# Rounded and low halves of weight chunks interleaved element by element for the stationary operand

## The chip, the cores and the metric

The kernel runs on one core of one Trainium2 chip. The metric is the device time of one execution in microseconds; lower is better. The chip multiplies on TensorE (PE in the profile), which loads a 128x128 stationary operand (the weight load, PEld) and then streams a moving operand of up to 512 columns past it. VectorE is DVE, ScalarE is ACT, GpSimd is POOL, and SyncE (SP) issues most transfers.

## The reference, cut to what matters

One decoder layer on 512 positions with a model width of 1024, in float32:

```python
h = rms_norm(x, norm1_g) * (1 + scale1) + shift1
z = h @ w_in      # [gMLP u | gMLP v | q | k | v | indexer q | indexer k | head weights | gate A | gate B]
y_a = chunked_gmlp(gelu(a_u), gelu(a_v), ...)
y_b = dsa_attention(q, k, v, qi, ki, wi)         # top-k keys of 512, 8 heads
merged = sigmoid(g_a) * (y_a @ w_proj_a) + sigmoid(g_b) * (y_b @ w_proj_b)
x = x + gate1 * (merged @ w_out)
h2 = rms_norm(x, norm2_g) * (1 + scale2) + shift2
f_g, f_u = split(h2 @ w_ffn_in)                   # 2 x 2816 columns
x = rms_norm(x + gate2 * ((silu(f_g) * f_u) @ w_ffn_out), final_norm_g)
```

The shifts, scales and gates are rows of `silu(c) @ w_ada + b_ada`.

## The kernel before, in words

Every large product is done in three passes to keep float32 accuracy. A float32 operand is split in a rounded half `hi` (a copy by ScalarE into the type fp32r) and a low half `lo` (the original minus `hi`, by VectorE or GpSimd). `mm3` then issues three matmuls: hi x hi, hi x lo and lo x hi, at lines 107, 108 and 109, so that these three lines carry nearly all matmuls, and a group of instructions is known by its tiles. In `mm3` the first pair is the stationary operand (128 columns are loaded), the second the moving one.

Weights come as a stream of chunks of 128 partitions x 1024 float32 (512 KB). `issue` starts the transfer of a chunk into one of three `raw` buffers, `prep` writes its halves into the next of three `hi` and three `lo` buffers (lines 156, 157, 163 and 167), and `get` and `ensure` hold the stream two chunks ahead of the matmuls. An entry of the stream is prepared in order. Among the weights stand rows of `w_ada` (`mod_row`, tile `mraw`): each is multiplied and summed on VectorE at line 255, and in the middle of the kernel all of them use one buffer.

The stages, in order of time, with the tiles that show in the rows:

- 16 to 49 us: eight chunks `W1` of 768 columns are stationary against `h`, six output tiles at a time (`k<-h`, `q<-h`, lines 606 to 610). Here GpSimd makes the low halves in pieces (line 165).
- 49 to 104 us: `W_Q` (`pb<-h`, by `opt_b`) with the chunk stationary and 384, later 512 columns of `h` moving; between them `W_VKI` (`pv`) with the chunk moving.
- 105 to 154 us: `W_AV` (`pav`), the chunk moving.
- 154 to 296 us: `W_AU`, `W_GA`, `W_PA` by `opt_b`, the chunk stationary, `h` or `y` moving (`pb<-h`, `pb<-y`). Beside it run the gMLP mixing (`mix`; `mix_ev` makes `y`), the top-k on VectorE (`sco`) and the `w_ada` rows.
- 297 to 370 us: attention, step by step (`at_step`), with the matmuls of `W_GB` (`pgb<-h`, chunk stationary) put between its steps.
- 371 to 414 us: `W_PB` (`pb<-yb`, chunk stationary), then the output projection (`po`).
- 457 to 671 us: the first FFN product by a Strassen-like scheme (`sprod`, tile `R`): 256 columns of `tb` or `h2` move, the chunk is stationary. Of the units `q`, the even ones take the buffers `hi` and `lo` three pairs at a time (`s_pair`), the odd ones other tiles (`sx`).
- 671 to 776 us: the second FFN product (`zprod`, tile `pfo`): the activations `za` are stationary, the chunk moves.

Where tiles lie is part of the design. All `raw`, `hi` and `lo` buffers before the change begin at 0 modulo 256 bytes of a partition, and so do `h`, `y`, `yb` and `za`. The moving operands of `sprod` are placed at 192 modulo 256 by `at_line(..., 192)`, its stationary ones lie at 0 or 128. `at_line` and small unused tiles (`fill`) hold these offsets.

Of the kernel before, what the change touches and what calls it, by code (L numbers as in the profile page):

```python
# [9 lines left out]
F32 = mybir.dt.float32  # L10
F32R = mybir.dt.float32r
# [5 lines left out]
S = 512  # L17
# [41 lines left out]
def block_kernel(ctx: ExitStack, tc: tile.TileContext, x, x_t, w_in,  # L59
# [3 lines left out]
    T, V, A, P, SY = nc.tensor, nc.vector, nc.scalar, nc.gpsimd, nc.sync  # L63
    ctx.enter_context(tc.manual_schedule())
    tiny = ctx.enter_context(tc.tile_pool(name="tiny", bufs=1))
    base = ctx.enter_context(tc.tile_pool(name="base", bufs=1))
# [6 lines left out]
    def packed(ap, name):  # L73
        at, o = {}, 0
        for k0, nk, cols_ in _plan()[name]:
            m = 128 * nk * sum(n for _, n in cols_)
            at[k0, nk, cols_] = slice(o, o + m)
            o += m
        return lambda k0, nk, cols_: ap[at[k0, nk, cols_]].rearrange("(p m) -> p m", p=128)

    w_in, w_ffn_in, w_ffn_out = (packed(*a) for a in ((w_in, "w_in"), (w_ffn_in, "w_ffn_in"), (w_ffn_out, "w_ffn_out")))
# [4 lines left out]
    def at_line(pool, tag, dims, dt, name, off=0):  # L86

        n = math.prod(dims)
        pad = 256 if tag == "E6" else (256 - HOME[tag]) % 256 or 192 if tag in HOME else 0
        t = pool.tile([128, n + pad // 4], dt, name=name, tag=tag, bufs=1)  # L90
        o = (off - HOME.get(tag, 0)) % 256 // 4
        letters = "abcd"[:len(dims)]
        return t[:, o:o + n].rearrange(f"p ({' '.join(letters)}) -> p {' '.join(letters)}",
                                       **dict(zip(letters[1:], dims[1:])))
# [4 lines left out]
    def f(ap):  # L99
        return ap.bitcast(F32)  # L100
# [11 lines left out]
    stream, wseq, chunk = [], [], {}  # L112
# [2 lines left out]
    last_raw = {}  # L115
    mrot = [0]

    def add_w(src, kts, c0, n, lo=None, where=None):
        stream.append(dict(kind="w", src=src, kts=kts, c0=c0, n=n, lo=lo or V, where=where))
        wseq.append(len(stream) - 1)  # L120
        return len(stream) - 1

    def add_m(dma, fn, early=False, mid=True):
        stream.append(dict(kind="m", fn=fn, dma=dma, early=early, mid=not early and mid))
        return len(stream) - 1
# [23 lines left out]
    def prep(i):  # L149
        e = stream[i]  # L150
        if e["kind"] == "m":
            e["fn"](e["raw"])
            return
        m = len(e["kts"]) * e["n"]
        if e["where"] is None:
            hi = base.tile([128, 1024], F32R, name="hi", tag="hi", bufs=3)
            lo = base.tile([128, 1024], F32R, name="lo", tag="lo", bufs=3)
        elif isinstance(e["where"], tuple):
            hi, lo = (at_line(base, t, (1024,), F32R, "wx") for t in e["where"])
        else:  # L160
            t = at_line(ffn[0], e["where"], (2, 1024), F32R, "wx", 128 * (e["where"] in ("E1", "E6")))
            hi, lo = t[:, 0], t[:, 1]
        A.activation(hi[:, :m], e["raw"][:, :m], AF.Copy)  # L163
        if e["lo"] == "later":
            e["do"] = lambda E=V, c=slice(0, m): E.tensor_sub(lo[:, c], e["raw"][:, c], f(hi[:, c]))
        else:
            e["lo"].tensor_sub(lo[:, :m], e["raw"][:, :m], f(hi[:, :m]))  # L167
        chunk[i] = (e["view"](hi), e["view"](lo))

    def ensure(upto):  # L170
        upto = min(upto, len(stream) - 1, st["limit"] - 1)
        while True:
            for i in range(st["prep"], min(st["prep"] + 16, len(stream), st["limit"])):
                if "raw" in stream[i]:
                    continue
                if room(i):
                    issue(i)
                elif stream[i]["kind"] == "w" or not stream[i]["mid"]:
                    break
            if st["prep"] > upto:  # L180
                break
            prep(st["prep"])
            st["prep"] += 1

    def room(i):
        e = stream[i]
        if i in last_raw:
            return True
        pend = [stream[k] for k in range(st["prep"], i) if k not in last_raw]
        if e["kind"] == "m" and e["early"]:  # L190
            return sum(p["kind"] == "m" for p in pend) < 8
        if e["kind"] == "m" and e["mid"]:
            return all(p["kind"] == "w" for p in pend) and len(pend) <= 1
        return sum(p["kind"] == "w" or not (p["early"] or p["mid"]) for p in pend) < RAWB


    def get(i, ahead=2):
        k = wseq.index(i)
        ensure(wseq[min(k + ahead, len(wseq) - 1)])
        return chunk[i]  # L200
# [10 lines left out]
    mid = mid_stack.enter_context(tc.tile_pool(name="mid", bufs=1))  # L211
# [5 lines left out]
    vmid = mid_stack.enter_context(tc.tile_pool(name="vmid", bufs=1))  # L217
    ffn = []

    for k in range(8):  # L220
        at_line(base, f"S2_{k}", (1024,), F32, "home")
    base.tile([128, 16], F32, name="fill")
    vmid.tile([128, 16], F32, name="fill")

    def s2pair(k, dt=F32R, name="s2"):
        return at_line(base, f"S2_{k}", (2, S), dt, f"{name}{k}")
# [51 lines left out]
    def group(src, c0, n=256, K=8, mods=None, pool=False, where=None, nm=1, mraw="A2"):  # L278
        ids = []
        for k0 in range(0, K, 4):  # L280
            ids.append(add_w(src, list(range(k0, min(K, k0 + 4))), c0, n,
                             P if pool == 2 or pool and k0 % 8 == 0 else V, where.pop(0) if where else None))
            for _ in range(nm if isinstance(nm, int) else nm[k0 // 4]):
                m = next(mods, None) if mods is not None else None
                if m is not None:
                    add_m(*m, mid=mods is mm_ and mraw)
        return ids

    W1M, W1 = [], []
    mods1 = [iter([mod_row(0, kt), mod_row(1, kt)]) for kt in range(8)]  # L290
    for c in "00w11w22w33w44w55w66w77w":
        if c == "w":
            W1.append(add_w(w_in, [len(W1)], ((3072, 256), (2048, 512)), 768, "later"))
        else:
            W1M.append(add_m(*next(mods1[int(c)]), True))
    W_Q = [group(w_in, 3584 + 256 * g) for g in range(2)]
# [100 lines left out]
    def x_kt(kt):  # L397
        return xts[kt // 4][:, kt % 4]
# [5 lines left out]
    for i in range(4):  # L404
        t = base.tile([128, D], F32, name=f"x{i}", tag=f"X{i}", bufs=1)
# [20 lines left out]
    def t512(name, dt=F32):  # L426
        return base.tile([128, 512], dt, name=name, tag="t512", bufs=3)
# [5 lines left out]
    def split(hi, lo, src):  # L433
        A.activation(hi, src, AF.Copy)
        V.tensor_sub(lo, src, f(hi))
# [74 lines left out]
    def stage_E(kt):  # L510
        g, sh, v = G1[:, 1, kt:kt + 1], G1[:, 0, kt:kt + 1], x_kt(kt) if kt else xp[0]
        if kt:
            A.activation(hT[kt][0], v, AF.Identity, scale=g, bias=sh)
        else:
            V.tensor_scalar(hT[kt][0], v, g, sh, op0=OP.mult, op1=OP.add)
        hf = hfs[kt] = t512("hf")
        A.activation(hf, v, AF.Identity, scale=g, bias=sh)
# [40 lines left out]
    def copy_x(c):  # L558
        for kt in (1, 2):
            A.activation(x_kt(kt)[:, c], xp[kt][:, c], AF.Copy)  # L560
# [12 lines left out]
    A.activation(rb, rbp, AF.Copy)  # L573
    copy_x(slice(256, 512))
    ensure(W1[0])
    stage_E(0)

    def low_w1(kt):
# [17 lines left out]
    for kt in range(8):  # L596
        hi, lo = chunk[W1[kt]]
# [5 lines left out]
        hh, hl = hT[kt]  # L603
# [93 lines left out]
    kin = mid.tile([128, 4, 128], F32, name="kin", tag="A2", bufs=1)  # L697
    wi = mid.tile([128, 4, 8], F32, name="wi")
    bst = vmid.tile([128, 4, 24], F32, name="bst", tag="L", bufs=1)
    mid.tile([128, 32], F32, name="fill")  # L700
    mv = tiny.tile([128, 4, 2], F32, name="mv")
    rki = sm[:, 8:12]

# [244 lines left out]
    for h in range(2):  # L948
        pb = [bank(k, "pav") for k in range(4)]
        for i in W_AV[h]:  # L950
# [10 lines left out]
            hi, lo = get(i)  # L961
# [328 lines left out]
    mT, om, ow, oraw = {}, {}, {}, {}  # L1290
# [11 lines left out]
    def o_w(key, src):  # L1302
        if key in OW:
            ow[key] = tuple((vmid if t[0] == "v" else mid).tile([128, 2, S], F32R, name="ow", tag=t, bufs=1)
                            for t in OW[key])
        else:
            ow[key] = tuple(base.tile([128, 2, S], F32R, name=t, tag=t, bufs=3) for t in ("hi", "lo"))
        split(*ow[key], oraw[src])

    def o_sub(o, a, b):  # L1310
# [24 lines left out]
    def pb_evac(g):  # L1335
        def ev(pb):
# [11 lines left out]
            if g == 2:  # L1348
                m_low(4)
        return ev  # L1350

    O_STEPS = [[lambda: o_w("B11", "B11")],
               [lambda: o_sub("B11", "B12", "B11")],
               [lambda: o_w("T1", "B11")],
# [103 lines left out]

    def s_pair(q, n):
        if q % 2 == 0:  # L1460
            return (base.tile([128, 4, 2, 128], F32R, name="hi", tag="hi", bufs=3),
                    base.tile([128, 4, 2, 128], F32R, name="lo", tag="lo", bufs=3))
        if n < 2:
            t = at_line(ffn[0], f"E{n}", (2, 4, 2, 128), F32R, "sx", 128 * (n == 1))
            return t[:, 0], t[:, 1]
        return tuple(at_line(base, f"S2_{2 + e}", (4, 2, 128), F32R, "sx") for e in range(2))
# [111 lines left out]
    for half in range(2):  # L1578
        for h in range(2):
# [5 lines left out]
            for n_, i in enumerate(W_O[2 * h:2 * h + 2]):  # L1585
                hi, lo = chunk[i]
# [158 lines left out]
    for half in range(2):  # L1745
        o = slice(half * 256, (half + 1) * 256)
        for w in range(2):
            for ci, i in enumerate(W_F[w]):
                hi, lo = chunk[i]
# [250 lines left out]
    for tk in range(2):  # L2000
        for z in range(2) if tk else (None,):
# [4 lines left out]
            n = c.stop - c.start  # L2006
# [78 lines left out]
```

## Time and profile before

| | before |
|---|---|
| median of the runs | 785.41 us |
| runs | 784.4 and 786.42 us |
| span of the profiled execution | 783.3 us |
| instructions in it | 12307 |

The span goes from the first to the last instruction of one profiled execution. The profile gives no other time for that execution: its own time is its span with what lies around it, and the two timed runs are 1.1 and 3.1 us longer than the span. A row of the timeline has start, length, engine, line, operation, tiles and count; the length of a matmul in it contains its way through the array, so the pace of matmuls is read from start to start, never from the lengths.

### The profile page before, as it was taken

The numbers are of one execution on the slowest core, as the hardware profiler recorded it, in microseconds if no ns is written. First come the engines' busy times: TensorE is split into PE (matmuls) and PEld (weight loads), VectorE is DVE, ScalarE is ACT, GpSimd is POOL, SyncE is SP. The second block draws the span as 40 slices with busy tenths as digits, with TensorE's granted clock in tenths as the row PEclk, the third lists the DMA queues.
The fourth block names the chain that finished last, engine by engine and source line by source line (L and its number), as shares of the span: only waits on it lengthen the run. The fifth ranks groups of instructions, "written<-read, shape, count | busy, mean of one in ns | idle before, by whom it ended". The sixth has DMA issues, their size and how long they took to land.

```text
span 783.3 us, 12307 instructions
## 1 busy us (share of the span) xinstructions
PE 774.1 (99%) x4579; PEld 688.5 (88%) x4579; DVE 666.6 (85%) x1128; ACT 427.3 (55%) x757; POOL 179.0 (23%) x234
## 2 busy tenths in 40 slices
PE   8999999999999999999999999999999999999996
PEld 7899888888888888988888899999999999888885
DVE  7989788887889559986697879989999888998877
ACT  6664445423332246666546577655566666676654
POOL 4870222312344412100020000313132223000001
PEclk8999999999999999999999999999999999999999
DMA  9953252332435558627682603879897967556762
GB/s 345 416 187 125 82 168 75 135 99 89 132 123 206 210 188 225 180 75 265 220 248 33 209 1 109 253 231 300 268 254 230 270 205 210 162 187 206 219 216 112
DMA packets 51277, 146.24 MB, mean 187 GB/s; under 512 B 13969, under 2 KB 14737, under 8 KB 51218
## 3 DMA queue, kind: packets, MB, share of 16 engines
q1 hardware_dynamic: 41408, 114.35, 42.2%
q0 software_dynamic: 9232, 30.15, 15.2%
q10 hardware_dynamic: 578, 0.95, 0.3%
q8 instruction: 36, 0.59, 0.3%
q14 instruction: 23, 0.19, 0.1%
HBM read 140.97 MB, written 27.27 MB: 215 GB/s over the span
## 4 chain that ended last, share of the span: by engine, by line
PE 81%; DVE 9%; DMA 6%; ACT 2%; issue 1%; SPq 0%; POOL 0%; POOLq 0%; DVEq 0%; ACTq 0%
PE R L107 8%; PE R L109 8%; PE R L108 8%; PE pb L108 5%; PE pb L109 5%; PE pb L107 5%; PE pfo L109 4%; PE pfo L107 4%; PE pfo L108 4%; DMA mraw<-in_w_shsc_dram 4%; DVE mraw L255 2%; PE pav L109 2%; PE pav L108 2%; PE pav L107 2%; PE po L109 2%; PE po L107 2%
## 5 line engine op out<-in xcount | busy, mean ns | idle before, releaser
L163 ACT ACTIVATE hi<-raw 128x1024 fp32r<-128x1024 f32 (+4 forms) x106 | 107.4, 1014 | 94.4 <-PE pb L108 38.9
L167 DVE TENSOR_TENSOR lo<-raw,hi 128x1024 fp32r<-128x1024 f32 (+2 forms) x73 | 85.4, 1171 | 24.0 <-ACT hi L163 23.6
L167 POOL TENSOR_TENSOR lo<-raw,hi 128x1024 fp32r<-128x1024 f32 x25 | 59.9, 2398 | 106.7 <-ACT hi L163 101.2
L107 PE MATMUL pb<-h,hi 128*128 128x512 f32 (+1 forms) x192 | 73.6, 383 | 0.0
L108 PE MATMUL pb<-h,hi 128*128 128x512 f32 (+1 forms) x192 | 73.0, 380 | 0.0
L109 PE MATMUL pb<-h,lo 128*128 128x512 f32 (+1 forms) x192 | 73.0, 380 | 0.0
L108 PE MATMUL pfo<-lo,za 128*128 128x512 f32 (+1 forms) x144 | 55.2, 383 | 0.0
L109 PE MATMUL pfo<-hi,za 128*128 128x512 f32 (+1 forms) x144 | 55.2, 383 | 0.0
L107 PE MATMUL pfo<-hi,za 128*128 128x512 f32 (+1 forms) x144 | 55.2, 383 | 0.0
L255 DVE CUSTOM_DVE_ANT_0 mraw<-mraw,csb,cols 128x1024 f32<-128x1024 f32 x27 | 39.3, 1455 | 18.6 <-DMA mraw<-in_w_shsc_dram 18.6
L389 POOL COPY sm<-sm 128x1 f32<-128x1 f32 x36 | 25.0, 696 | 92.3 <-ACT sm L388 92.2
L107 PE MATMUL R<-tb,hi 128*128 128x256 f32 x160 | 44.2, 276 | 0.0
L108 PE MATMUL R<-tb,hi 128*128 128x256 f32 x160 | 44.2, 276 | 0.0
L109 PE MATMUL R<-tb,lo 128*128 128x256 f32 x160 | 44.2, 276 | 0.0
L107 PE MATMUL R<-tb,sx 128*128 128x256 f32 x160 | 44.2, 276 | 0.0
L108 PE MATMUL R<-tb,sx 128*128 128x256 f32 x160 | 44.2, 276 | 0.0
L109 PE MATMUL R<-tb,sx 128*128 128x256 f32 x160 | 44.2, 276 | 0.0
L109 PEld LDWEIGHTS pb<-h,lo 128*128 128x128 f32 x192 | 36.0, 188 | 6.3
L108 PEld LDWEIGHTS pb<-h,hi 128*128 128x128 f32 x192 | 36.1, 188 | 6.0
L107 PEld LDWEIGHTS pb<-h,hi 128*128 128x128 f32 x192 | 36.1, 188 | 6.0
L369 POOL DMA_DIRECT2D wsum<-in_w_ffn_out_dram x24 | 19.6, 822 | 72.3 <-DMA wsum<-wsum 39.7
L108 PEld LDWEIGHTS pfo<-lo,za 128*128 128x128 f32 x144 | 27.1, 188 | 5.4
(395 smaller groups left out, 2563.2 us busy)
## 6 DMA issues: line engine op xcount, KB each, us to landing
raw<-in_w_ffn_in_dram SPq DMA_DIRECT2D x44, 512.0 KB
raw<-in_w_in_dram SPq DMA_DIRECT2D x40, 512.0 KB
wsum<-in_w_ffn_out_dram POOLq DMA_DIRECT2D x30, 512.0 KB, 7.5
mraw<-in_w_shsc_dram SPq DMA_DIRECT2D x27, 512.0 KB
raw<-wsum SPq DMA_DIRECT2D x20, 512.0 KB
s<-in_w_shsc_dram SPq DMA_DIRECT2D x14, 512.0 KB
raw<-in_w_ffn_out_dram SPq DMA_DIRECT2D x13, 512.0 KB
wsum<-wsum POOLq DMA_DIRECT2D x10, 512.0 KB, 5.9
```

The lines of the kernel that those rows point to most:

```text
L107: T.matmul(o, wh, rh, start=start, stop=False, **kw)
L108: T.matmul(o, wh, rlo, start=False, stop=False, **kw)
L109: T.matmul(o, wlo, rh, start=False, stop=stop, **kw)
L163: A.activation(hi[:, :m], e["raw"][:, :m], AF.Copy)
L167: e["lo"].tensor_sub(lo[:, :m], e["raw"][:, :m], f(hi[:, :m]))
L255: V.tensor_tensor_reduce(out=raw[:, c], in0=raw[:, c], in1=(csb if s > 1 else pc)[:, c], scale=scale, scalar=sums.pop(0), op0=OP.mult, op1 ...
L369: P.dma_start(wsum_at(n, c), src, max_dma_last_dim=4096, accum_op=OP.add)
L389: P.tensor_copy(t, t)
```

## The change

The three `hi` and three `lo` buffers become three buffers `hl` of 2048 elements with 16 more as padding (8256 bytes, that is 64 more than a multiple of 256), so that they begin at 0, 64 and 128 modulo 256. For chunks that are marked `still` (those of `W1` and of `group`, when they go through these buffers) `hi` has the even and `lo` the odd elements: an engine that writes or reads a half steps by 8 bytes, and a weight load reads 128 elements over 1024 bytes where it read 512 bytes. For all others `hi` is the first and `lo` the second 1024 elements of a buffer. Small unused tiles are moved so that later tiles of the pool keep their offsets.

```diff
+    def pair_tile():
+        return base.tile([128, 2064], F32R, name="hl", tag="hl", bufs=3)[:, :2048]
+
-    def add_w(src, kts, c0, n, lo=None, where=None):
+    def add_w(src, kts, c0, n, lo=None, where=None, still=False):
...
         if e["where"] is None:
-            hi = base.tile([128, 1024], F32R, name="hi", tag="hi", bufs=3)
-            lo = base.tile([128, 1024], F32R, name="lo", tag="lo", bufs=3)
+            t = pair_tile()
+            if e["still"]:
+                t = t.rearrange("p (m e) -> p m e", e=2)
+                hi, lo = t[:, :, 0], t[:, :, 1]
+            else:
+                hi, lo = t[:, :1024], t[:, 1024:]
...
     base.tile([128, 16], F32, name="fill")
-    vmid.tile([128, 16], F32, name="fill")
...
             ids.append(add_w(src, list(range(k0, min(K, k0 + 4))), c0, n,
-                             P if pool == 2 or pool and k0 % 8 == 0 else V, where.pop(0) if where else None))
+                             P if pool == 2 or pool and k0 % 8 == 0 else V, where.pop(0) if where else None, True))
...
-            W1.append(add_w(w_in, [len(W1)], ((3072, 256), (2048, 512)), 768, "later"))
+            W1.append(add_w(w_in, [len(W1)], ((3072, 256), (2048, 512)), 768, "later", still=True))
...
     ensure(W1[0])
+    base.tile([128, 16], F32, name="fill2")
...
-    mid.tile([128, 32], F32, name="fill")
+    mid.tile([128, 16], F32, name="fill")
...
-            ow[key] = tuple(base.tile([128, 2, S], F32R, name=t, tag=t, bufs=3) for t in ("hi", "lo"))
+            t = pair_tile().rearrange("p (e j n) -> p e j n", e=2, j=2)
+            ow[key] = (t[:, 0], t[:, 1])
...
         if q % 2 == 0:
-            return (base.tile([128, 4, 2, 128], F32R, name="hi", tag="hi", bufs=3),
-                    base.tile([128, 4, 2, 128], F32R, name="lo", tag="lo", bufs=3))
+            t = pair_tile().rearrange("p (h j e n) -> p h j e n", h=2, j=4, e=2)
+            return t[:, 0], t[:, 1]
```

## Rows read from the trace of the kernel before

**Rows 1.** The page: busy time by engine, and the chain that ended last.
```profile
PE 774.1 (99%) x4579; PEld 688.5 (88%) x4579; DVE 666.6 (85%) x1128; ACT 427.3 (55%) x757; POOL 179.0 (23%) x234
...
PE 81%; DVE 9%; DMA 6%; ACT 2%; issue 1%; SPq 0%; POOL 0%; POOLq 0%; DVEq 0%; ACTq 0%
```

**Rows 2.** Timeline of PE, 40.7 to 42.2 us, inside stage W1.
```profile
40.76 0.61 PE L606 MATMUL k<-h,hi 128*128 128x512 f32 x2
...
42.12 0.61 PE L608 MATMUL k<-h,lo 128*128 128x512 f32 x2
```

**Rows 3.** Windows: stretch, its us, each engine's busy us (instructions), PEclk, DMA, GB/s.
```profile
16.00:49.00 33.00, 33.00 (x145) 27.05 (x146) 29.21 (x41) 20.92 (x31) 29.81 (x49) 1.00 0.91 358
49.00:66.00 17.00, 17.00 (x100) 17.00 (x99) 16.66 (x30) 9.18 (x16) 5.75 (x12) 1.00 0.43 137
154.00:182.50 28.50, 28.50 (x132) 23.76 (x131) 23.82 (x39) 8.59 (x11) 5.94 (x4) 1.00 0.26 89
182.50:310.00 127.50, 127.50 (x594) 106.64 (x592) 100.57 (x226) 47.71 (x74) 44.81 (x26) 1.00 0.51 171
310.00:372.00 62.00, 61.86 (x376) 54.91 (x375) 51.81 (x155) 40.96 (x104) 6.06 (x12) 1.00 0.56 180
372.00:414.00 42.00, 42.00 (x187) 34.79 (x186) 34.07 (x44) 18.48 (x25) 5.65 (x10) 1.00 0.73 228
482.00:671.00 189.00, 189.00 (x1670) 189.00 (x1669) 174.17 (x237) 115.49 (x235) 48.19 (x74) 1.00 0.81 237
```

**Rows 4.** Timeline of PE near the end: 256 columns move, both operands at 0.
```profile
774.37 0.28 PE L107 MATMUL pfo<-hi,za 128*128 128x256 f32 x1
...
775.81 0.28 PE L107 MATMUL pfo<-wx,zl 128*128 128x256 f32 x1
```

**Rows 5.** Groups of weight loads by form: count, busy us, mean ns, idle before.
```profile
L107 PEld LDWEIGHTS pb<-h,hi 128*128 128x128 f32 x192 | 36.1, 188 | 6.0
...
L107 PEld LDWEIGHTS pfo<-hi,za 128*128 128x128 f32 x144 | 27.1, 188 | 5.3
...
L107 PEld LDWEIGHTS pgb<-h,hi 128*128 128x128 f32 x64 | 12.1, 188 | 2.5 <-ACT gb L1220 0.6
...
L107 PEld LDWEIGHTS pb<-y,hi 128*128 128x128 f32 x64 | 12.0, 188 | 2.4
...
L107 PEld LDWEIGHTS pb<-yb,hi 128*128 128x128 f32 x64 | 12.0, 188 | 2.5
...
L606 PEld LDWEIGHTS q<-h,hi 128*128 128x128 f32 x32 | 6.0, 188 | 1.3
...
L606 PEld LDWEIGHTS k<-h,hi 128*128 128x128 f32 x16 | 2.8, 188 | 1.1 <-ACT h L513 0.4 <-issue 0.3
```

**Rows 6.** The chain that ended last, in order of time, 182 to 311 us.
```profile
182.50 0.91 PE mix L984 x8
183.43 0.70 DVE y L990
...
227.18 4.30 DMA mraw<-in_w_shsc_dram
...
231.50 1.29 DVE mraw L255
...
309.84 0.56 ACT gb L1220
...
310.44 0.50 PE pgb L107
```

**Rows 7.** Groups that write or read the halves, by form: count, busy us, mean ns.
```profile
L163 ACT ACTIVATE hi<-raw 128x1024 fp32r<-128x1024 f32 x89 | 94.0, 1058 | 85.6 <-PE pb L108 38.9 <-PE pfo L109 18.6 <-issue 14.5
...
L167 DVE TENSOR_TENSOR lo<-raw,hi 128x1024 fp32r<-128x1024 f32 x64 | 78.1, 1221 | 23.1 <-ACT hi L163 22.8
...
L167 POOL TENSOR_TENSOR lo<-raw,hi 128x1024 fp32r<-128x1024 f32 x25 | 59.9, 2398 | 106.7 <-ACT hi L163 101.2 <-PE pb L108 4.5 <-POOL sco L768 0.9
...
L165 POOL TENSOR_TENSOR lo<-raw,hi 128x384 fp32r<-128x384 f32 x8 | 8.0, 1017 | 2.4 <-ACT hi L163 2.4
```

More of the change, by code (lines that the diff above doesn't have):

```diff
@@ L116, in block_kernel @@
     mrot = [0]
-    def add_w(src, kts, c0, n, lo=None, where=None):
-        stream.append(dict(kind="w", src=src, kts=kts, c0=c0, n=n, lo=lo or V, where=where))
+    def pair_tile():
+        return base.tile([128, 2064], F32R, name="hl", tag="hl", bufs=3)[:, :2048]
+    def add_w(src, kts, c0, n, lo=None, where=None, still=False):
+        stream.append(dict(kind="w", src=src, kts=kts, c0=c0, n=n, lo=lo or V, where=where, still=still))
         wseq.append(len(stream) - 1)
```

## The prediction

> **What bounds the kernel now.** I read the page first: TensorE is busy 99% of the span and holds 81% of the chain that ended last; VectorE has 9% of it and transfers 6% [rows 1]. So the first question is what sets TensorE's pace, and that is read from starts, not from lengths. In stage W1 six matmuls of 512 columns start between 40.76 and 42.12 us, 226.7 ns each [rows 2]. The granted clock there is 1.00, which is the level of 2.4 GHz [rows 3], and 512 columns at one column per cycle are 213.3 ns. Each matmul is 13.3 ns, or 32 cycles, over its columns. The same is seen with 256 columns (106.7 ns): near the end of the kernel, with both operands at 0 modulo 256 bytes, twelve matmuls take from 774.37 to 775.81 us, 120 ns each, again 13.3 over [rows 4]; in `sprod`, where the moving operand lies at 192, the stretch from 482 to 671 us holds 1670 in 189 us, 113.2 ns each, only 6.5 over [rows 3]. The two have the same number of columns, the same clock and the same kind of weight load. What differs is the address of the moving operand against that of the weights loaded beside it. I read this as two streams that meet in the same part of the memory: the moving one goes 4 bytes per cycle; a weight load of 128 columns fits into 113 ns in `sprod`, so it goes at about half of that, and the moving stream keeps overtaking it.
>
> The second question is where TensorE's pace sets the end. Up to the mixing at 182.50 us the chain is TensorE's; from the `y` at 183.43 on it runs through VectorE and the `mraw` transfers (4.30 us of transfer, then 1.29 us of line 255, and so on) and comes back to TensorE only at the `pgb` of 310.44, which had waited for ScalarE [rows 6]. That wait is 0.6 us in all [rows 5]. So from 182.5 to 310 us two chains are equally long: TensorE is busy in all 127.5 us [rows 3], but the other would not be shorter if it were faster.
>
> **The change part by part.** *The interleaved weight load.* It reads 1024 bytes in the time in which it read 512, so it moves at the bytes per cycle of the moving stream. Two streams of one speed don't overtake each other: they are apart for the whole load, or one is held once and they are apart after that. From the rows a matmul then costs between nothing and one meeting over its columns. The nearest row for one meeting is `sprod`'s 6.5 ns [rows 3], so the saving lies between 6.7 and 13.3 ns per matmul. With three buffers at three distances from the moving operand, which lies at 0, I expect some of each and take the middle, 10 ns, that is a pace of about 217 ns. The unseen lower end, a load that gets more expensive, is a rival below.
>
> The Trainium skill has a rule against this reading. "SBUF — State Buffer", section "Who interferes with whom", says that TensorE has two independent read ports, one for the moving operand and one for weight loads, and that only the port pair shared by VectorE and GpSimd causes contention. By it the 13.3 ns would be no meeting and the change would save nothing; that is the second rival. The trace's 120 against 113.2 ns for equal work speaks against it [rows 3, 4].
>
> The matmuls concerned are the weight loads of line 107 or 606 times three: 192 `pb<-h`, 64 `pgb`, 64 `pb<-y`, 64 `pb<-yb`, 32 `q` and 16 `k`, 432 in all, hence 1296 [rows 5]. By stage, at 10 ns each:
> - W1: 48 x 3 = 144 matmuls, 1.4 us. But the transfers there are at a share of 0.91 and GpSimd is busy 29.8 of 33 us [rows 3], so I count half, 0.7 us.
> - `W_Q`: by its loop 4 x 8 x 2 x 3 = 192, 1.9 us. VectorE has 17.0 - 16.7 = 0.3 us left in the first 17 us [rows 3], but the work is spread on to 104 us.
> - `W_AU` until 182.5 us: 132 instructions less a mixing of 8 and the edges [rows 3], some 120, 1.2 us.
> - 182.5 to 310 us: some 510, 5.1 us on TensorE, nothing at the end: `y` and `mraw` are late next, and TensorE will wait for them.
> - 310 to 372 us: of the 192 `pgb` some 145, 1.4 us. VectorE is busy 51.8 of 62 us between the steps of attention [rows 3]; I count 1.1 us.
> - `W_PB`: 64 x 3 = 192 in 42 us, where VectorE has 8 us to spare [rows 3], 1.9 us.
>
> The sum is 0.7 + 1.9 + 1.2 + 1.1 + 1.9 = 6.8 us.
>
> *The writes with a step of 8 bytes.* No row shows one. The contiguous ones take 1058 ns on ScalarE, 1221 on VectorE, 2398 on GpSimd for 1024 columns, and 1017 on GpSimd for 384 [rows 7]: each takes roughly the same time per element whatever the length, which looks like one element at a time, so I take them as unchanged. The upper bound is a doubling. It would add 1.2 us to each low half on VectorE, 16 of them in `W_Q` and `W_PB` where 0.3 to 8 us are free, and about 1 us to each piece on GpSimd in W1, where 3.2 us are free [rows 3]. Below nothing is excluded: a wider step makes no engine faster. GpSimd's later low halves (25 of 2398 ns) are hidden: it waits 106.7 us before them [rows 7].
>
> *One buffer for both halves.* ScalarE's write of a chunk three places on waits for the end of the last matmul that reads the buffer; this was line 108 for `hi` (38.9 us of ScalarE's waits in all [rows 7]) and becomes line 109, one matmul or 0.23 us later. Behind it on ScalarE stand the next evacuations, on VectorE or GpSimd the low half. The stream is two chunks, or 48 matmuls and 11 us, ahead, which covers it; without this cover it would cost 0.23 us for each of some 50 chunks.
>
> *The other users of the buffers.* In `sprod` ten even units of 6 products of 12 matmuls, 720, load weights from the buffers: now a third each at 0, 64 and 128. Against a moving operand at 192, 0 and 128 are distances that the 113.2 ns already contains [rows 3]; 64 is a distance of half of 256, which no row shows. The bounds are 113.2 and 120 ns [rows 3, 4], and a saving of as much is not excluded: 240 x 6.7 ns = 1.6 us either way. I take +0.8 us, because two operands at distance 0 were the worst and half of 256 may be the same if the pattern repeats twice in it. In `zprod` (144 x 3 matmuls [rows 5]) and `W_AV` and `W_VKI` the chunk moves, two thirds of them now at 64 or 128 against weights at 0. A matmul of 512 columns lasts about twice as long as the load beside it, so I expect all meetings to fall inside it at any distance: nothing. The bounds are 13.3 and 6.7 ns over, 400 x 6.7 = 2.7 us of gain. `o_w` and the moved filling tiles add no instruction; I put them at nothing.
>
> Net: 6.8 - 0.8 = 6.0 us. The profiled execution has no time but its span, 783.3 us, which becomes 777.3; the median of 785.41 lies 2.1 us above the span, so 779.4. I predict **779.3 us**, 0.8% less. A measurement of this kernel can tell about 2% from no change.
>
> **The rivals.** *Each byte of weights costs (slower).* If the 13.3 ns come not from overtaking but from every stretch of memory that a load touches (512 bytes cost 32 cycles), a load over 1024 bytes costs 26.7 ns. It decides as soon as a load costs more than 13.3 ns, and then everywhere, since TensorE is busy all the time in each of these stages [rows 3]: 1296 x 13.3 = 17.3 us, 803 us. For it speaks that the excess is the same for 256 and 512 columns [rows 2, 4]; against it that `sprod`'s loads, of as many bytes, cost half [rows 3]. The Trainium skill ("SBUF — State Buffer", section on the DMA port swizzle) says that two accesses to one line of 16 bytes suffice for full bandwidth. A step of 8 bytes just has them, so by that rule the load isn't longer; no row shows it.
>
> *No saving.* The excess belongs to each pair of load and matmul, whatever the addresses, or the meetings stay because both streams keep together in the same part: 785, at most 1.6 us to either side from `sprod`. Against it stands the difference between rows 3 and rows 4.
>
> *More saving.* From 182.5 to 310 us the other chain gives way too (its 4.30 us transfers are partly queueing behind chunks [rows 6]), and all 1296 matmuls save 10 to 13.3 ns: 13 to 17 us, 768 to 772. Against it: VectorE's 1.29 us and its transfer follow one another in one buffer.
>
> *Slow writes eat it.* If 8-byte steps slow the engines, W1 and `W_Q` become theirs: 3 to 8 us against the 6 of gain, 782 to 788.
>
> **How the numbers follow.** Forecast (776 to 782): 0.45. No saving (783.5 to 787): 0.22. Weights by the byte (790 to 804): 0.13. More saving (768 to 776): 0.10. Slow writes: 0.10. The range from 772 to 790 leaves out the third and half of the fourth, 0.18. Below 769.7 (faster by 2%) lies about a third of the fourth, 0.04; above 801.1 some two thirds of the third, 0.09; within 2%, 0.87. For the forecast alone the range is 776 to 782.
>
> **What would show it.** Right: `k`, `q` and `pb` start every 213 to 220 ns, N = 384 likewise 7 to 13 ns sooner; the first `mix` of the chain comes 3 to 5 us earlier; TensorE gets idle time between 182 and 310 us, ended by `y` or `mraw`; `pfo` keeps its 227 ns. Wrong: a pace of 240 ns; lines 163 and 167 longer than 1.06, 1.22 and 2.4 us for interleaved chunks; a pace that changes but an unchanged arrival at 310 us; `R` far from 113 ns.

## The result and the profile after

The kernel after takes 796.0 us (795.89 and 796.11) where the kernel before took 785.41: ratio 1.0137, 95% interval 1.0105 to 1.0169. The profiled span is 794.2 us against 783.3. The forecast was 779.3 with a range from 772 to 790: the change was to save 6 us and costs 11, and the time lies outside the range.

The page of the kernel after, busy time by engine and the chain, against [rows 1]:

```profile
PE 785.2 (99%) x4579; PEld 699.8 (88%) x4579; DVE 668.3 (84%) x1128; ACT 432.7 (54%) x757; POOL 179.0 (23%) x234
...
PE 80%; DVE 10%; DMA 5%; ACT 2%; issue 1%; SPq 0%; POOLq 0%; POOL 0%; DVEq 0%; ACTq 0%
```

TensorE is busy for 11.1 us more with as many matmuls, and the span grew by 10.9. So nothing new is waited for; matmuls got slower. How much, the timeline says, in W1 (six matmuls of 512 columns, compare [rows 2]) and at the end (256 columns, compare [rows 4]):

```profile
41.48 0.63 PE L616 MATMUL k<-h,hl 128*128 128x512 f32 x2
41.94 1.09 PE L616 MATMUL q<-h,hl 128*128 128x512 f32 x4
42.88 0.63 PE L618 MATMUL k<-h,hl 128*128 128x512 f32 x2
...
785.12 0.28 PE L107 MATMUL pfo<-wx,zl 128*128 128x256 f32 x1
...
786.56 0.28 PE L107 MATMUL pfo<-hl,za 128*128 128x256 f32 x1
```

From 41.48 to 42.88 us six matmuls start, 233.3 ns each where it was 226.7. The twelve matmuls from 785.12 to 786.56 still take 120 ns on average. Nine of them move chunks from two neighbouring buffers, of which at least one no longer lies at 0, and the starts of these nine are 117 to 127 ns apart where each was 120. The windows, with the columns of [rows 3]:

```profile
16.00:49.00 33.00, 33.00 (x145) 27.64 (x144) 27.41 (x41) 21.90 (x31) 29.97 (x48) 1.00 0.92 358
49.00:66.00 17.00, 17.00 (x99) 17.00 (x98) 16.73 (x30) 9.11 (x15) 5.13 (x11) 1.00 0.40 125
154.00:182.50 28.50, 28.50 (x129) 23.99 (x128) 23.02 (x37) 9.47 (x12) 4.59 (x4) 1.00 0.27 93
182.50:310.00 127.50, 127.50 (x581) 107.84 (x580) 100.48 (x219) 46.81 (x67) 44.98 (x22) 1.00 0.49 163
310.00:372.00 62.00, 61.75 (x373) 55.60 (x372) 53.01 (x155) 41.17 (x105) 7.99 (x16) 1.00 0.58 183
372.00:414.00 42.00, 42.00 (x186) 35.15 (x184) 33.61 (x48) 21.03 (x29) 5.40 (x9) 1.00 0.75 238
482.00:671.00 189.00, 189.00 (x1639) 189.00 (x1639) 172.82 (x239) 112.25 (x227) 41.96 (x69) 1.00 0.79 232
```

The clock is 1.00, the level of 2.4 GHz, in every stage, so it isn't the cause. In the last row 1639 matmuls stand where 1670 stood: 115.3 ns each in `sprod` for 113.2. In the row from 182.5 to 310 us 581 stand for 594.

The weight loads by form, as in [rows 5]:

```profile
L107 PEld LDWEIGHTS pb<-h,hl 128*128 128x128 f32 x192 | 37.4, 195 | 5.8
...
L107 PEld LDWEIGHTS pfo<-hl,za 128*128 128x128 f32 x144 | 27.0, 188 | 5.6
...
L107 PEld LDWEIGHTS pgb<-h,hl 128*128 128x128 f32 x64 | 12.5, 195 | 2.4 <-ACT gb L1228 0.7
```

An interleaved load's record is 195 ns for 188. `pfo`, where the chunk moves and `za` is loaded, keeps 188, and its matmuls are slower all the same (table below). The chain in order of time, against [rows 6]:

```profile
183.93 0.91 PE mix L992 x8
184.85 0.70 DVE y L998
...
228.76 3.67 DMA mraw<-in_w_shsc_dram
...
314.10 0.49 ACT gb L1228
314.63 0.51 PE pgb L107
```

The mixing comes 1.4 us later (I had expected 3 to 5 earlier), `pgb` 4.2 later. The profile still draws the chain between them through VectorE and the `mraw` transfers. The writers of the halves, against [rows 7]:

```profile
L170 ACT ACTIVATE hl<-raw 128x1024 fp32r<-128x1024 f32 x89 | 98.1, 1104 | 89.8 <-PE pb L109 39.6 <-PE pfo L109 23.2 <-issue 20.0
...
L174 DVE TENSOR_TENSOR hl<-raw,hl 128x1024 fp32r<-128x1024 f32 x64 | 78.1, 1221 | 24.8 <-ACT hl L170 24.3
...
L174 POOL TENSOR_TENSOR hl<-raw,hl 128x1024 fp32r<-128x1024 f32 x25 | 60.8, 2433 | 109.5 <-ACT hl L170 108.6 <-POOL sco L776 0.9
```

VectorE and GpSimd write with a step of 8 bytes at nearly their old speed (1221 ns as before; 2433 for 2398). ScalarE gained 4.1 us over the 48 interleaved chunks among its 89, 85 ns each; it is busy 54% of the span, and the account below needs nothing from it.

**The account by group.** Both kernels issue the same matmuls in the same order, so the mean from start to start can be compared group by group:

| group (matmuls) | before, ns | after, ns | us in all |
|---|---|---|---|
| `k` and `q` (144) | 230.7, 228.1 | 234.2, 231.9 | +0.54 |
| `pb<-h`, 384 columns (96) | 173.6 | 175.7 | +0.20 |
| `pb<-h`, 512 columns (480) | 228.2 | 233.4 | +2.48 |
| `pb<-y` (192) | 227.2 | 231.9 | +0.91 |
| `pgb` (192) | 236.7 | 240.0 | +0.63 |
| `pb<-yb` (192) | 226.8 | 231.7 | +0.94 |
| `R` from the buffers, `hl` (720) | 113.3 | 116.7 | +2.47 |
| `R` from tiles that the change didn't touch, `sa`, `sx` (960) | 113.3 | 114.5 | +1.13 |
| `pfo`, 512 columns (447) | 226.7 | 230.9 | +1.90 |
| `pav` (192), `pv`, `po` | 227.6 for `pav` | 230.4 for `pav` | +0.89 |
| the start of the kernel | | | -1.0 |

The sum is 11.1 us. Interleaved chunks lose 5.7 of it; 6.4 are lost where nothing is interleaved; the start of the kernel, before any chunk is multiplied, was 1.0 shorter.

### The profile page after: what moved, and what is told of

Read it like the earlier page. It is cut to its first block, busy times and chain, and to the rows that moved or that the text cites. A ratio compares the mean times of both kernels' runs of the same rounds, so it can differ in the third digit from the quotient of the medians.

```text
span 794.2 us, 12306 instructions
## 1 busy us (share of the span) xinstructions
PE 785.2 (99%) x4579; PEld 699.8 (88%) x4579; DVE 668.3 (84%) x1128; ACT 432.7 (54%) x757; POOL 179.0 (23%) x234
## 4 chain that ended last, share of the span: by engine, by line
PE 80%; DVE 10%; DMA 5%; ACT 2%; issue 1%; SPq 0%; POOLq 0%; POOL 0%; DVEq 0%; ACTq 0%
PE R L107 8%; PE R L108 8%; PE R L109 8%; PE pb L108 5%; PE pb L109 5%; PE pb L107 5%; PE pfo L107 4%; PE pfo L109 4%; PE pfo L108 4%; DMA mraw<-in_w_shsc_dram 4%; DVE mraw L262 3%; PE pav L108 2%; PE pav L109 2%; PE pav L107 2%; PE po L109 2%; PE po L108 2%
## 5 line engine op out<-in xcount | busy, mean ns | idle before, releaser
L170 ACT ACTIVATE hl<-raw 128x1024 fp32r<-128x1024 f32 (+4 forms) x106 | 112.0, 1058 | 101.6 <-PE pb L109 39.6
L174 DVE TENSOR_TENSOR hl<-raw,hl 128x1024 fp32r<-128x1024 f32 (+2 forms) x73 | 85.4, 1171 | 25.8 <-ACT hl L170 25.3
L174 POOL TENSOR_TENSOR hl<-raw,hl 128x1024 fp32r<-128x1024 f32 x25 | 60.8, 2433 | 109.5 <-ACT hl L170 108.6
L107 PE MATMUL pb<-h,hl 128*128 128x512 f32 (+1 forms) x192 | 74.4, 388 | 0.0
L108 PE MATMUL pb<-h,hl 128*128 128x512 f32 (+1 forms) x192 | 73.8, 384 | 0.0
L109 PE MATMUL pb<-h,hl 128*128 128x512 f32 (+1 forms) x192 | 73.8, 384 | 0.0
L262 DVE CUSTOM_DVE_ANT_0 mraw<-mraw,csb,cols 128x1024 f32<-128x1024 f32 x27 | 41.6, 1541 | 18.9 <-DMA mraw<-in_w_shsc_dram 18.9
L107 PE MATMUL pfo<-hl,za 128*128 128x512 f32 (+1 forms) x144 | 56.0, 389 | 0.0
L109 PE MATMUL pfo<-hl,za 128*128 128x512 f32 (+1 forms) x144 | 55.7, 387 | 0.0
L108 PE MATMUL pfo<-hl,za 128*128 128x512 f32 (+1 forms) x144 | 55.4, 385 | 0.0
L108 PE MATMUL R<-tb,hl 128*128 128x256 f32 x160 | 44.7, 279 | 0.0
L107 PE MATMUL R<-tb,hl 128*128 128x256 f32 x160 | 44.6, 279 | 0.0
L109 PE MATMUL R<-tb,hl 128*128 128x256 f32 x160 | 44.6, 279 | 0.0
L396 POOL COPY sm<-sm 128x1 f32<-128x1 f32 x36 | 23.3, 647 | 86.6 <-ACT sm L395 86.5
L109 PEld LDWEIGHTS pb<-h,hl 128*128 128x128 f32 x192 | 37.4, 195 | 6.0
L107 PEld LDWEIGHTS pb<-h,hl 128*128 128x128 f32 x192 | 37.4, 195 | 5.8
L108 PEld LDWEIGHTS pb<-h,hl 128*128 128x128 f32 x192 | 37.4, 195 | 5.8
L109 PEld LDWEIGHTS pfo<-hl,za 128*128 128x128 f32 x144 | 27.0, 188 | 6.1
```

The costliest lines, as they stand in the source:

```text
L107: T.matmul(o, wh, rh, start=start, stop=False, **kw)
L108: T.matmul(o, wh, rlo, start=False, stop=False, **kw)
L109: T.matmul(o, wlo, rh, start=False, stop=stop, **kw)
L262: V.tensor_tensor_reduce(out=raw[:, c], in0=raw[:, c], in1=(csb if s > 1 else pc)[:, c], scale=scale, scalar=sums.pop(0), op0=OP.mult, op1 ...
L396: P.tensor_copy(t, t)
```

## The experiments

Two theories stood after the result. One: the interleaving itself slows the load, and the places of the buffers are a detail. The other: the pace hangs on the distance between weights and moving operand, so the spread of the three buffers costs, with or without interleaving. The first two runs part them.

**Interleaved, all buffers at 0.** Edit against the kernel after:

```diff
-        return base.tile([128, 2064], F32R, name="hl", tag="hl", bufs=3)[:, :2048]
+        return base.tile([128, 2048], F32R, name="hl", tag="hl", bufs=3)
...
-    base.tile([128, 16], F32, name="fill2")
```

> The halves stay interleaved, but the three buffers are 2048 elements without padding, so all begin at 0 modulo 256. If the step of 8 bytes is what costs in the matmuls with a stationary chunk, k, q, pb and pgb start about every 233 ns as they do in the changed kernel for the buffer at 0 (226.7 before), some 1200 x 6.3 ns = 7.5 us, while R goes back to 113.3 and pfo to 226.7 ns: about 792 to 793 us. If the spread of the buffers over 0, 64 and 128 is what costs and interleaving by itself is free or a gain, pb is at 226.7 ns or below and the time is 785 us or less.

Measured: 791.58 us, ratio 1.0091 (1.0073 to 1.0109), span 789.6. `pb` and `q` with 512 columns start every 233 to 235 ns (`pb<-yb` 233.3, `pb<-h` 234.7), the 384-column ones every 173.3 as before. `R` and `pfo` have their old 113.3 and 226.7. So interleaving loses with all buffers at 0: 6.7 ns at 512 columns, nothing at 384. The chain of this run, on its page:

```profile
PE 97%; DMA 1%; DVE 1%; SPq 0%; issue 0%; ACT 0%; POOLq 0%; POOL 0%; DVEq 0%
```

TensorE held 81% of it before [rows 1]. The whole stretch from 182.5 to 310 us now goes by TensorE and no longer by VectorE: the slower TensorE has become the longer of the two chains that were equal before.

**Contiguous halves, buffers spread over 0, 64 and 128.** Edit against the kernel after:

```diff
-            if e["still"]:
+            if False:
```

> No interleaving: hi is the first and lo the second half of each buffer for all chunks; the buffers begin at 0, 64 and 128 as in the changed kernel. If the step of 8 bytes costs only in the matmuls with a stationary chunk, pb goes back to 226.7 ns and R (116 to 117) and pfo (224 to 236, mean some 231) stay slow: +5 to 6 us over before, 790 to 791 us. If the spread is the whole cause, pb stays at about 231 ns too and the time is that of the changed kernel, 795 to 796 us.

Measured: 795.46 us, 1.0135 (1.012 to 1.015), span 793.8. Without one interleaved element a loss of the same size is there: `pb<-h` 232.1 ns, `pb<-yb` 231.0, `pfo` 230.9, `R` as in the kernel after. The two parts of the change don't add: spread alone +10.9 us, interleaving alone +7.0, both +10.6.

**One offset at a time.** All three buffers at 64 or at 128; for 64, against the kernel after (the pairs for 128 have 32 and 32 elements of filling; the contiguous ones the edit above as well):

```diff
-        return base.tile([128, 2064], F32R, name="hl", tag="hl", bufs=3)[:, :2048]
+        return base.tile([128, 2048], F32R, name="hl", tag="hl", bufs=3)
...
+    base.tile([128, 16], F32, name="fill1")
     ensure(W1[0])
-    base.tile([128, 16], F32, name="fill2")
+    base.tile([128, 48], F32, name="fill2")
```

Contiguous at 64: 

> No interleaving, all three buffers at 64 modulo 256: one constant distance between moving and stationary operand, other than 0. If mixing several distances is what breaks a steady pace, pb, R and pfo each have one constant pace; with meetings that depend on the distance it is 120 ns for R (distance of half of 256) and between 220 and 233 for pb and pfo. If any offset but 0 costs, pb and pfo are at 229 to 233 and R at 118: 793 us or more.

Measured: 801.83 us, 1.0216 (1.0199 to 1.0234).

Interleaved at 64: 

> Interleaved, all three buffers at 64 modulo 256. If loads of one speed with the moving operand keep apart at some distance, pb is below 226.7 ns here or in the run with all buffers at 0, at a constant pace. If the step of 8 bytes costs by itself, pb is at 229 to 234 ns, as for the buffer at 64 in the changed kernel (228 to 235), and the time lies 5 us or more above the same placement without interleaving.

Measured: 799.59 us, 1.0191 (1.0175 to 1.0206).

Contiguous at 128: 

> No interleaving, all three buffers at 128 modulo 256. Weights at 128 under a moving operand at 192 is what sa and sx already have: by the distance alone, or by a pattern that the offset 64 breaks, R is at 113.3 ns throughout; if any departure from the offsets of before breaks the pattern, R is at 117 to 118. pb and pfo, at a distance of 128, are at 226.7 if the pattern of 512 columns repeats within 256 bytes, else at 229 to 233; 785 to 797 us.

Measured: 795.0 us in one run, beside one of 784.33 of the kernel before.

Interleaved at 128: 

> Interleaved, all three buffers at 128 modulo 256. At 0 the interleaved pace was 233 ns, at 64 it was 230 to 233. If a load over 1024 bytes costs by itself, it is 228 ns or more here as well; if two streams of one speed keep apart at this distance, 220 ns or less.

Measured: 794.17 us in one run.

The paces, from start to start, in ns:

| | `pb<-yb` (buffer loaded, moving at 0) | `pfo` (buffer moves, weights at 0) | `R<-tb,hl` (buffer loaded, moving at 192) | `R<-tb,sx` (untouched, weights at 0 and 128) |
|---|---|---|---|---|
| before, all at 0 | 226.8 | 226.7 | 113.3 | 113.3 |
| contiguous at 64 | 233.3 | 228.9 | 118.8 | 117.9 |
| contiguous at 128 | 233.3 | 233.3 | 113.3 | 113.5 |
| interleaved at 0 | 233.3 | 226.7 | 113.3 | 113.5 |
| interleaved at 64 | 230.1 | 228.9 | 118.8 | 117.9 |
| interleaved at 128 | 231.4 | 233.3 | 113.3 | 113.3 |

Each offset has a pace of its own, and no cell is faster than before. I had expected interleaving at 64 to take 5 us or more over the contiguous halves there, if the step of 8 bytes costs by itself; it takes 2.2 us less. So the step has no fixed price: it loses at 0 (233.3 for 226.7) and gains at 64 (230.1 for 233.3). `sprod` loses at 64 only, and there `sx` loses too, whose addresses are the old ones. The same stretch in four of these runs shows it by its count of matmuls; in order, interleaved at 0, spread, contiguous at 64, contiguous at 128:

```profile
482.00:671.00 189.00, 189.00 (x1670) 189.00 (x1669) 174.85 (x242) 114.38 (x235) 43.13 (x71) 1.00 0.82 237
```
```profile
482.00:671.00 189.00, 189.00 (x1640) 189.00 (x1639) 172.90 (x240) 112.21 (x228) 48.33 (x70) 1.00 0.81 233
```
```profile
482.00:671.00 189.00, 189.00 (x1604) 189.00 (x1603) 169.73 (x236) 110.47 (x223) 45.09 (x67) 1.00 0.79 231
```
```profile
482.00:671.00 189.00, 189.00 (x1669) 189.00 (x1669) 174.94 (x242) 114.36 (x234) 43.19 (x71) 1.00 0.81 236
```

**A map of the pace.** A kernel with nothing but blocks of 36 matmuls, moving operand and weights each at 0, 64, 128 or 192 (a, b, c, d in the names), its core:

```python
for c in range(count):
    g, j = (c // 3) % 4, c % 3
    T.matmul(p[:, :n], w(g, j // 2), (hi, lo, hi)[j], start=c == 0, stop=c == count - 1)
```

> The work of the layer is left out: the kernel only streams matmuls from tiles in SBUF, in blocks of 36 (as mm3 does: hi x hi, hi x lo, lo x hi), for 512 and 256 columns, loads of step one (512 bytes) and step two (1024 bytes), moving operand at 0, 64, 128, 192 (a to d) and weights at 0 to 192, all blocks once forwards and once backwards, and then the fast pair of offsets with three matmuls of another offset put in. No other engine works beside it. If the pace depends on the distance alone, a block has the same pace forwards and backwards and the fast pair returns to 113.3 and 226.7 ns at once after the three. If TensorE keeps a pattern, the fast pair stays at 117 to 118 and 229 to 231 ns after the three matmuls, and blocks differ by what ran before them. If VectorE and ScalarE, writing their halves at 64, were what slowed the units whose own operands did not move, no block here shows it. If loads of one speed keep apart at some distance, some block of step two is below 226.7 ns; if a load over 1024 bytes costs by itself, all of them are at 228 ns or more.

Measured: the four combinations with the same distance (weights less moving operand, modulo 256) agree. In ns:

| distance | 512 columns, step one | 512, step two | 256, step one | 256, step two |
|---|---|---|---|---|
| 0 | 226.7 | 233.3 | 120.0 | 119.8 to 120.0 |
| 64 | 233.3 | 230.0 | 113.3 or 117.8 | 119.9 to 120.1 |
| 128 | 232.2 to 232.4 | 231.5 | 118.4 to 118.8 | 120.0 to 121.2 |
| 192 | 228.9 | 233.3 | 113.3 or 117.8 | 119.9 to 120.1 |

The timeline of this kernel, of the blocks of step one with distances 64, 128, 192, 192 and 0, and later of step two with 0, 64, 128 and 192 (the last row of each part only ends the block before it):

```profile
23.62 8.56 PE L66 MATMUL n_ma_sb_one<-mov,sta 128*128 128x512 f32 x36
32.02 8.53 PE L66 MATMUL n_ma_sc_one<-mov,sta 128*128 128x512 f32 x36
40.39 8.41 PE L66 MATMUL n_ma_sd_one<-mov,sta 128*128 128x512 f32 x36
48.64 8.42 PE L66 MATMUL n_mb_sa_one<-mov,sta 128*128 128x512 f32 x36
56.89 8.33 PE L66 MATMUL n_mb_sb_one<-mov,sta 128*128 128x512 f32 x36
65.06 8.56 PE L66 MATMUL n_mb_sc_one<-mov,sta 128*128 128x512 f32 x36
...
148.20 8.56 PE L66 MATMUL n_ma_sa_two<-mov,sta 128*128 128x512 f32 x36
156.60 8.44 PE L66 MATMUL n_ma_sb_two<-mov,sta 128*128 128x512 f32 x36
164.88 8.50 PE L66 MATMUL n_ma_sc_two<-mov,sta 128*128 128x512 f32 x36
173.22 8.56 PE L66 MATMUL n_ma_sd_two<-mov,sta 128*128 128x512 f32 x36
181.62 8.56 PE L66 MATMUL n_mb_sa_two<-mov,sta 128*128 128x512 f32 x36
```

Read from start to start: 8.40 us from the first row to the second, over 36, is 233.3 ns; 8.17 from the row at 56.89 is 227; 8.28 from the row at 156.60 is 230. No other engine works beside these blocks, so neither writes nor transfers make the difference. With 512 columns every block has the same pace when the blocks are run backwards, and distance 0 returns to 226.7 ns after three matmuls of another offset. One thing has two values: with 256 columns at distances 64 and 192 a block runs at 113.3 or at 117.8 throughout. A sequence at the end of the kernel shows that the addresses don't decide between them:

```profile
822.34 4.40 PE L66 MATMUL n_md_sa_one<-mov,sta 128*128 128x256 f32 x36
826.59 0.51 PE L66 MATMUL n_md_sb_one<-mov,sta 128*128 128x256 f32 x3
826.93 7.23 PE L66 MATMUL n_md_sa_one<-mov,sta 128*128 128x256 f32 x60
834.00 4.40 PE L66 MATMUL n_md_sc_one<-mov,sta 128*128 128x256 f32 x36
838.24 4.25 PE L66 MATMUL n_md_sa_one<-mov,sta 128*128 128x256 f32 x36
842.32 0.53 PE L66 MATMUL n_md_sa_two<-mov,sta 128*128 128x256 f32 x3
842.68 6.97 PE L66 MATMUL n_md_sa_one<-mov,sta 128*128 128x256 f32 x60
```

The same block `n_md_sa_one` takes 7.07 us for 60 matmuls (117.8 ns) from 826.93, and after another block between them 4.08 us for 36 (113.3) from 838.24. The same is seen in `sprod` of the kernel after, in the first rows of four of its products of twelve matmuls:

```profile
496.33 0.28 PE L107 MATMUL R<-h,sa 128*128 128x256 f32 x1
497.75 0.28 PE L107 MATMUL R<-tb,sx 128*128 128x256 f32 x1
...
506.01 0.28 PE L107 MATMUL R<-h,sa 128*128 128x256 f32 x1
507.37 0.28 PE L107 MATMUL R<-tb,hl 128*128 128x256 f32 x1
```

The product `sa` from 496.33 us, at addresses of old and right behind six products from the buffers, takes 1.42 us for its twelve (118 ns); the next `sa`, from 506.01, takes 1.36 (113). In the run with all buffers at 64, whose six products from the buffers stand at distance 128 (118.8 ns), all that follow stay in the slower pattern. In the kernel before no product of `sprod` stands at that distance. So a product at distance 128 seems to throw TensorE out of the faster pattern, but it isn't the only thing that does. The map has a slow block right behind a fast one, both at distance 64:

```profile
328.70 4.26 PE L66 MATMUL n_mc_sd_one<-mov,sta 128*128 128x256 f32 x36
332.80 4.40 PE L66 MATMUL n_md_sa_one<-mov,sta 128*128 128x256 f32 x36
```

And in the next run, without any product at distance 128, the matmul of `sprod` that starts at 492.28 us is followed by the next only after 0.15 us, and the 71 behind it run at 117.8 ns.

**The common buffer alone.** Both edits together, all buffers at 0, contiguous:

```diff
-        return base.tile([128, 2064], F32R, name="hl", tag="hl", bufs=3)[:, :2048]
+        return base.tile([128, 2048], F32R, name="hl", tag="hl", bufs=3)
...
-            if e["still"]:
+            if False:
...
-    base.tile([128, 16], F32, name="fill2")
```

> Both halves of a chunk in one buffer, contiguous, all three buffers at 0: only the common buffer and the moved filling tiles are left of the change. Theory (spread and interleaving are the whole loss): 785 us, ratio 1.000 with at most 0.002 to either side, pfo every 226.7 ns, R every 113.3 ns, k and q as before (230.7 and 228.1). Rival (the common buffer's later release is part of the loss that the runs with spread or interleaving showed): 787 to 790 us, with longer waits of ScalarE ahead of the copy into hl.

Measured: 784.95 us, 0.9998 (0.9989 to 1.0008); `q` 227.5, `pb<-yb` 226.8, `R` 113.5 ns (the slow stretch just named is the 0.2), `pfo` as before. The common buffer, its later release and the moved filling cost nothing that these ten runs can show; spread and interleaving are the whole loss.

**Step and offset.** The same kind of kernel with a step of one, two and four elements and finer offsets:

```python
return W[:, c:c + 128 * step].rearrange("p (m e) -> p m e", e=step)[:, :, half]
```

> The layer is left out; the matmuls run alone, blocks of 36, the moving operand at 0, weights at offsets from 0 to 320 bytes with a step of one, two or four elements, for 512, 384 and 128 columns. Theory (the offset modulo 256 sets the pace, the load's span in bytes adds to it): step one 226.7 ns at 0 and 256, 233.3 at 64 and 320, 232 at 128, 229 at 192; 16 and 32 between 0 and 64; step two 233.3, 230, 231.5 and 233.3 at 0, 64, 128 and 192; step four slower again, 240 ns or more at 0. Rival 1 (only the part of 64 bytes decides): step one at 64, 128, 192 and 256 the same. Rival 2 (a wider step costs once, whatever its width): step four at 230 to 233 ns like step two. For 384 columns the same excess in ns over 160 as 512 has over 213.3; for 128 columns the load sets the pace and the offset does nothing.

Measured, in ns from the seventh matmul of a block on, 512 columns (the granted clock is 1.00 in all blocks named here):

| offset | 0 | 16 | 32 | 64 | 96 | 128 | 160 | 192 | 224 | 256 | 320 |
|---|---|---|---|---|---|---|---|---|---|---|---|
| step one | 226.7 | 226.7 | 233.4 | 233.4 | 234.3 | 232.7 | 233.2 | 228.8 | 233.2 | 226.7 | 233.4 |
| step two | 235.6 | 233.5 | 231.7 | 229.9 | 233.3 | 231.4 | 233.3 | 233.4 | 233.6 | 233.3 | 230.1 |
| step four | 235.1 | 233.3 | 237.5 | 238.3 | 235.7 | 240.0 | 233.3 | 239.8 | 236.7 | 234.9 | 238.3 |

At step one the pace repeats with 256 bytes, as the theory had it. At step two offset 0 gives 235.6 where 256 gives 233.3, as the map gave at distance 0: here too one distance has two paces. By step one, rival 1 falls, since 64, 128 and 192 differ from 256. The theory's other half falls as well: with step four I had put 240 ns or more at offset 0, and it is 235.1, no more than step two. Rival 2 isn't right either, since step four reaches 240 at other offsets. At 384 columns and offset 0, steps one, two and four take 173.3, 173.3 and 233.3 ns, and at 128 columns, where the load is the longer part, steps one and two take 111.7 and 117.8 (up to 120.0 at other offsets). With 384 columns and step one, offsets 64, 128 and 192 give 176.7, 176.1 and 173.3: not the excess of 512 columns, as I had expected. Windows of this kernel over the five blocks of 36 at offset 0, in that order (the counts contain neighbours that reach in):

```profile
293.66:299.92 6.26, 6.26 (x37) 6.25 (x36) 0.00 (x0) 0.00 (x0) 0.00 (x0) 1.00 0.01 3
318.85:325.09 6.24, 6.24 (x37) 6.24 (x37) 0.00 (x0) 0.00 (x0) 0.00 (x0) 1.00 0.01 3
344.01:352.42 8.41, 8.41 (x38) 8.41 (x37) 0.00 (x0) 0.00 (x0) 0.00 (x0) 1.00 0.00 0
377.63:381.60 3.97, 3.97 (x38) 3.97 (x37) 0.00 (x0) 0.00 (x0) 0.00 (x0) 1.00 0.00 0
393.66:397.90 4.24, 4.24 (x39) 4.24 (x38) 0.00 (x0) 0.00 (x0) 0.00 (x0) 1.00 0.00 0
```

An interleaved load alone is 6 to 8 ns longer than a contiguous one and is hidden behind 160 ns of moving columns, yet 512 columns lose 6.7 to 8.9 at offset 0. So the loss isn't the load's length. With step four (the third window, 8.41 us for 36) the pace of 384 columns is 233.3 ns instead of 173.3: there the load itself has become the longer part.

## Why the prediction was wrong

**The step that failed** is this: "Two streams of one speed don't overtake each other: they are apart for the whole load, or one is held once and they are apart after that. From the rows a matmul then costs between nothing and one meeting over its columns." The premise held roughly: the load reads 1024 bytes in 118 to 120 ns where it read 512 in 111.7. The conclusion didn't. Over eleven offsets an interleaved load gives no pace under 229.9 ns: the smallest excess over the columns is 16.6 ns, where it was to lie between nothing and 6.5, and where the kernel before has 13.3. The rows that had led to it, 120 ns at distance 0 against 113.2 at distances 64 and 192 [rows 3, 4], do show an effect of the distance, but for 256 columns; I carried it over to 512, where distance 0 is the best place (226.7), 192 costs 2.2 ns more and 64 costs 6.6. One row of another length was no measure of the direction.

**The stages.** I counted -6.8 us; the groups show +5.7. (My sum gives 779.4 us where I wrote 779.3, a slip without weight.) The 182.5 to 310 us stretch, counted at nothing for a gain, isn't nothing for a loss: both chains were equally long, so a slower TensorE lengthens the stretch at once. From the mixing (+1.4 us) to `pgb` (+4.2) it lost 2.8 us. By TensorE's starts its interleaved matmuls there make some 2.5 of these; its wait for `gb` is 0.7 us where it was 0.6. That the profile still draws the chain through VectorE says only that the two chains ended together again; with interleaving at 0 it goes through TensorE.

**Other users.** "I expect all meetings to fall inside it at any distance: nothing" failed as well: chunks that move at 64 and 128 against weights at 0 stand at distances 192 and 128, which cost 2.2 and 5.5 to 6.6 ns a matmul of 512 columns in the map and in the runs with one offset. `zprod`, `W_AV` and the output projection lost 2.6 us, against a bound that was drawn on the side of a gain alone (`pv`'s 0.2 is there in the run interleaved at 0 too, so it isn't the distance). The map doesn't give all of it: the mean of 226.7, 228.9 and 233.3 is 229.6 for `pfo`, measured 230.9. For `sprod` I had +0.8 with bounds of 1.6 to either side; it lost 3.6. The place was right (64 under 192, that is half of 256) and so was the direction. The size was off: a third of 720 at 118.8 for 113.3 gives 1.3 us, and the other 2.3 fell on products at distances that the kernel before has too, left in the slower pattern, which no row of that kernel shows.

**What held.** The common buffer at nothing (0.9998), writes on VectorE unchanged and on GpSimd nearly so, and the clock. `pfo` at 256 columns hardly moved (119.0 ns for 119.7 on average), but at 512 it did not keep its 227 ns.

**The rivals.** "Each byte of weights costs" had the sign and a price of 13.3 ns; the interleaving costs 6.7 at offset 0, gains 3.3 at distance 64 and costs nothing at 384 columns and offset 0, so its mechanism falls with its size. Its sign was right by luck. "No saving" and "more saving" are out; "slow writes" too, but for ScalarE's 85 ns, which the sum by groups doesn't need. None of the four had the spread as a cost of its own, and the run with the spread alone has a ratio of 1.0135 where both parts have 1.0137.

**Ports and lines.** In the map only weights and moving operand are read, and the weights' place alone moves the pace from 226.7 to 233.3 ns. The Trainium skill ("SBUF — State Buffer", section "Who interferes with whom") has TensorE's two read ports independent of each other. The map doesn't agree: the places matter. What follows from that rule, that the change saves nothing, still came nearer to the result than my reading of the rows. The rule of the Trainium skill on lines of 16 bytes ("SBUF — State Buffer", section on the DMA port swizzle: two accesses to a line for full bandwidth) agrees within some 8 ns: steps one and two load in 111.7 and 117.8 to 120.0 ns, step four, with one access per line, paces 384 columns at 233.3. The 6.7 ns that 512 columns lose don't follow from it.

**What stays open** is why a distance has its pace, why interleaving costs 512 columns 6.7 ns at offset 0 and 384 columns none, and what in the order of the matmuls picks one of the two patterns. How buffers at different distances act on each other in one kernel was not tried in parts: the 1.3 ns of `pfo` over the mean of the three are not explained.

## What to carry to other kernels

The place of a stationary operand against the moving one, modulo 256 bytes, is worth 3% of a TensorE-bound stage at 512 columns (226.7 to 233.3 ns) and 6% at 256 (113.3 to 120.0); it is measured at the kernel's own column count, since 256 and 512 columns prefer different distances. Before operands are moved, list everyone who uses the same buffers: more than half of the loss here came from products that the change didn't mean. And where two chains are equally long, a loss in one counts in full (2.8 us here); that a gain in one would be worth nothing was assumed, and no run shows it.

## What the runs showed of the hardware that was not expected

- With 512 columns and contiguous weights the best distance is 0 (226.7 ns); 32 to 160 bytes cost 5.5 to 7.6 ns more, 192 costs 2.2, 224 costs 6.5, and 256 is 0 again. A shift of 16 bytes costs nothing.
- With 256 columns distance 0 is the worst (120.0), and distances 64 and 192 have two lasting paces, 113.3 and 117.8 ns, for the same addresses; which one runs depends on what ran before.
- Reading the stationary operand with a step of 8 bytes costs 512 columns 6.7 ns at distance 0 and saves 3.3 at distance 64.
- A stationary operand read with a step of 8 bytes loads nearly as fast as a contiguous one (117.8 to 120.0 against 111.7 ns from start to start at 128 columns); with a step of 16 bytes it paces matmuls of 384 columns at 233.3.
